# Weight splits, landing places and fill shares in the second layer of a two-layer decoder trunk

## The chip, the cores and the metric

The kernel runs on one core of one Trainium2 chip. The metric is the device time of one execution, in microseconds (us); lower is better. The engines are named as in the profile: PE is TensorE, ACT is ScalarE, DVE is VectorE, POOL is GpSimd, SP is SyncE, which only issues DMAs here.

## The reference

The trunk has two layers over 1024 tokens of width 1024. Each layer computes `LayerNorm(alpha * x + W_out [main * silu(gate); memory * silu(gate)])`. Layer 0's main branch is multi-scale pooling; layer 1's is "forgetting attention" (FoX), which takes nearly half of the time:

```python
def forgetting_attention(u, k, v, cum):       # 16 heads of 64, 1024 x 1024 causal
    logits = q . k * 64 ** -0.5 + (cum[t] - cum[s])   # cum: running sum of log-sigmoid forget gates
    return softmax(where(s <= t, logits, -inf)) . v

def mixer_sublayer(x, mem, w_in, w_mem_kv, w_out, main_fn):
    h = x @ w_in                               # main | memory queries | main gate | memory gate
    y_main, y_mem = main_fn(...), memory_attention(...)     # 4 heads over 256 memory tokens
    y = concat([y_main * silu(g_main), y_mem * silu(g_mem)])
    return y @ w_out                           # w_out is 1536 x 1024
```

Keys, values and forget gates of FoX come from one projection of layer 0's output. Everything is float32 at the borders.

## The kernel before, in words

**Precision.** A float32 product is made of three products of halves: high x high, and the two mixed ones. So every operand is *split*: one engine casts it to the high half, another subtracts to get the low half. `scaled_hi_lo` does it for the projections of layer 1 (high half on ACT, line 171; low half on DVE, line 172, both float16); `hi_lo` does it for the output projection (high half on ACT, line 197; low half on DVE, line 198; a bfloat16 copy of the high half on ACT, line 199). A weight piece first lands in a buffer called `raw` by a DMA on SP's queue.

**Order.** PE runs in the written order (`manual_schedule`). The instructions of the other engines and of the DMA queue are placed by the framework's scheduler, except those that are pinned (`keep_in_program_order`, passed around as `pin`), which keep the written order. Whatever its place, an instruction waits for its data and for the buffer that it writes.

**Start of FoX.** `start_units` computes the values of the first pairs and the forget-gate logits (`v_first`, eight blocks, matmuls on line 845, evacuated on lines 852 to 854), then a long chain of small instructions on DVE (`forget_gates`, lines 863 to 876), and beside it the projections of the first pair (`own`: keys, then queries) and of the second (`following`: keys first). Their matmuls are on line 356, their evacuations on lines 907 and 908. The cumulated gates are matmuls on line 884 that need the end of the chain.

**FoX.** `fox` goes over 16 heads, and in each over `ST` = 8 steps, one step for each tile of 128 queries, longest first, so step k has 128 x (8 - k) keys. A step of 640 keys or more has two parts. The logits are matmuls on line 324 into one of three banks `L`; DVE takes the bank's contents on line 1004 (mask, gates, running minimum); ACT makes exponentials (line 1012); the halves of P are made on ACT (line 1040) and DVE (line 1041); a DMA on SP transposes them to `T` (line 1057), and `values` multiplies them with V (line 1066) `LAG` = 6 steps later. After head 15 come six more steps ("head 16") with values only.

**Fill.** While DVE and ACT work on a step, PE is given other matmuls, the *fill*: the projections of later pairs, and of gates (line 356, with the tanh of a gate on line 372). `fill.pump(columns)` issues some of it. The share of a step is worked out so that steps are of planned lengths: each step's own logits (2 x 128 x (8 - k) columns) are allowed for, corrected by the table `MORE`; steps 1 and 5, where values are computed, by `VALUES`. A share is pumped in two parts (`FRAC` = 0.4, 0.6).

**Evacuating values.** `values` returns a function `out`, which evacuates the bank `O` (ACT line 1086, DVE line 1087) and lets POOL multiply by the gate and SP write to `y1d` in DRAM. `fox` keeps these in `outs`: for one half of a head it is called in the same step, for the other two steps later.

**Output projection.** `OutProj` takes W_out of layer 1 in 24 pieces of 128 x 512. `fetch_two` gets two of them into room that is free anyway, `fetch` gets one into a `raw` buffer; `split` splits in order, fetching first what has not been fetched. Pieces 0 to 7 are fetched during heads 14 and 15; pieces 8 to 11 at the first step of head 16, into `raw`; pieces 12 to 15 and the rest as they are split. Pieces 8 to 13 are split in the last three steps of head 16, pinned; the rest in `rest`. `late_gate` loads the outputs of some pairs back from `y1d` into a buffer `R`, multiplies them by the gate (POOL, line 1113) and writes them again (line 1114); pair 6 is the last. `rest` loads y in pieces (line 631, `T<-y1d`), splits them, and does the products (line 596).

`lines[0]` is a buffer of 16 rows of 1024 float16 numbers per partition; in layer 1 keys and queries of a pair are in its rows 0 to 6 or 8 to 14, by the pair's parity.

Of the kernel before, what the change touches and what calls it, by code (L numbers as in the profile page):

```python
# [9 lines left out]
F32 = mybir.dt.float32  # L10
# [4 lines left out]
AF = mybir.ActivationFunctionType  # L15
ALU = mybir.AluOpType
AX = mybir.AxisListType

P = 128
# [3 lines left out]
ST = S // P  # L23
NH = 512
HEADS = 16
# [12 lines left out]
PSCALE = 2.0 ** 15  # L38
QKSCALE = 2.0 ** -17
VALUES = {1: 39 * P, 5: 15 * P}  # L40
MORE = (-800, 2330, 1130, 410, -310, -70, -1270, -1420)


class Fill:
# [34 lines left out]
def trunk_kernel(ctx, tc, x, xT, memT, win, wk, wv0, wv, wmk, wmv, wout, poolw, pscale, lng, lnb, bforget, out):  # L79
# [90 lines left out]
    def scaled_hi_lo(to, src, sc, pin=lambda ins: ins):  # L170
        pin(nc.scalar.activation(to.hi, src, AF.Copy, scale=sc))  # L171
        pin(nc.vector.scalar_tensor_tensor(to.lo, src, sc, to.hi, ALU.mult, ALU.subtract))
# [32 lines left out]

    roomy = []

    pinned_w = [False]

    def split_w(src_dram, shape, sc=None, r=None):  # L210
        if r is None:
            r = raw(shape)
            nc.sync.dma_start(r, src_dram)
        if sc is not None:
            to = half_of(wt, shape)
            if low[0]:
                gp_scaled_hi_lo(to, r, sc)
            else:
                scaled_hi_lo(to, r, sc, tc.keep_in_program_order if pinned_w[0] else lambda ins: ins)
            return to  # L220
        to = parts_of(wt, shape)
        (gp_hi_lo if low[0] else hi_lo)(to, r)
        return to
# [317 lines left out]
    class OutProj:  # L541
# [8 lines left out]
        def fetch_two(self, land):  # L550

            n = self.n + len(self.raws)
            for j in range(2):
                nc.sync.dma_start(land[:, j, :], wout[self.l, n // 2 % 2, 2 * self.KKS[n // 4] + j])
                self.raws.append(land[:, j, :])

        def fetch(self, upto):

# [233 lines left out]
    X = X1  # L792
    with tc.tile_pool(name="in1", bufs=1) as in1:
# [4 lines left out]
        def land(shape):  # L798
            return sb(list(shape), "B", 10, F32, in1)
# [35 lines left out]
        def v_first():  # L835

            ws = first_ws
            first_vs.extend(vt([P, 2, 2 * ST, 64], F16) for _ in range(2))
            for s in range(ST):
                acc = ps([P, NH], "pj", 2)  # L840
                parts = (1, 2, 0) if s % 2 else (0, 2, 1)
                for i in parts:
                    for kt in range(KT):
                        u, w = three(X[:, kt, s * P : (s + 1) * P], ws[kt // 4][:, kt % 4, :])[i]
                        nc.tensor.matmul(
                            acc[:, :FW], u, w, start=kt == 0 and i == parts[0], stop=kt == KT - 1 and i == parts[2],
                        )
                        yield FW
                for pr in range(2):
                    of = acc[:, pr * P : (pr + 1) * P].rearrange("p (b d) -> p b d", b=2)  # L850
                    hi, lo = (first_vs[pr][:, :, 2 * s + e, :] for e in range(2))
                    nc.scalar.activation(hi, of, AF.Copy, scale=QKSCALE)
                    nc.vector.scalar_tensor_tensor(lo, of, QKSCALE, hi, ALU.mult, ALU.subtract)
                nc.vector.scalar_tensor_tensor(
                    flog[:, s * HEADS : (s + 1) * HEADS], acc[:, 2 * P : FW], un1s[1], bfb, ALU.mult, ALU.add,
                )

        def forget_gates():

# [50 lines left out]
        own_ws = []  # L910

        def own_weights():
            own_ws.extend(split_w(wk[0, pc], [P, 4, P], sws[1]) for pc in range(2))

        def k_units(p):

            own, odd = (lines[0][:, k : k + 2, :] for k in (8 * (p % 2), 8 * (p % 2) + 2))

            def evac(cols, acc):
                halves_out(own[:, 0], own[:, 1], cols, acc, QKSCALE)  # L920
                if cols.stop == S:
                    move((odd, high64, own, high64), (odd, low64, own, high64), (own, high64, own, low64))

            yield from slab(wk[p] if p else own_ws, X, evac, g=1)
            pairs[p] = [[(own[:, 0], own[:, 1]), (odd[:, 0], odd[:, 1])]]

        def q_units(p):

            a, b, c = (lines[0][:, 8 * (p % 2) + k, :] for k in (4, 5, 6))

            def evac(cols, acc):
                halves_out(a, b, cols, acc, -QKSCALE)
                if cols.stop == S:
                    move((c, low64, a, high64), (c, high64, b, high64), (a, high64, b, low64))

            yield from slab(win[1, p], X, evac, g=1)
# [16 lines left out]

        def start_units(own, following):

            pinned_w[0] = True
            yield from v_first()
            gates = forget_gates()
            next(gates)
            yield from islice(own, 58)  # L960
            next(gates)
            yield from islice(own, 9)
            next(gates)
            yield from own
            yield from islice(following, 48)
# [93 lines left out]
        def values(hd, c, o, gs):  # L1059

            v, un, b = pairs[hd // 2][2], unv if hd >= 4 else unv0, hd % 2
            acc = ps([P, NH], "O", 1)
            blocks = [(i, j) for i in range(4 * c, 4 * c + 4) for j in range(i + 1)]

            def add(rows, i, j, e, first, last):
                nc.tensor.matmul(  # L1066
                    acc[rows, (i % 4) * P : (i % 4) * P + P], v[:, b, 2 * j : 2 * j + (1 if e else 2), :].rearrange("p e d -> p (e d)"),
                    pt[hd, i][:, e * (i + 1) + j, :], start=first, stop=last,
                )
# [12 lines left out]
            oc = o[own, c * NH : (c + 1) * NH]  # L1082

            def out():

                nc.scalar.activation(oc, acc[other, :], AF.Copy, scale=un[own])
                nc.vector.scalar_tensor_tensor(oc, acc[own, :], un[own], oc, ALU.mult, ALU.add)
                if b:
                    pair_out(hd // 2, c, o, gs.get(hd // 2))

            return out

        bfb = const.tile([P, HEADS], F32, name="bfb")
        nc.sync.dma_start(bfb, bforget.partition_broadcast(P))
# [20 lines left out]

        def fox(following, out_proj):
            fill, past, fresh = Fill(), [None] * LAG, [None]
            gs, outs = {}, []

            def gate_ahead(pr):  # L1120
                gs[pr] = G()
# [5 lines left out]
            for hd in range(HEADS + 1):  # L1127
# [16 lines left out]
                for i in range(ST if hd < HEADS else LAG):  # L1144
# [1 line left out]
                    last = ST + LAG if hd == HEADS else (hd | 1) * ST + ST  # L1146
                    at = ST if hd == HEADS else hd * ST
                    todo = [VALUES.get(k % ST, 0) if k >= ST else 0 for k in range(at + i, last)]
                    if hd < HEADS:
                        for n, k in enumerate(range(at + i, min(last, HEADS * ST))):  # L1150
                            todo[n] += 2 * P * (ST - k % ST) - MORE[k % ST]
                    part = max(0, (fill.left + sum(todo)) / len(todo) - todo[0])
                    new, split = None, []

# [16 lines left out]
                    if pr == 7:  # L1171
                        step = b * ST + i
                        if step in (0, 1, 5, 11):
                            out_proj.fetch_two(land((P, 2, NH)))
                        if step == 9:
                            lead = out_proj.early(land((P, 4, 2 * P)), parts_of(xy, (P, 4, 2 * P)))
                            next(lead)
                    if hd == HEADS and i == 0:
                        out_proj.fetch(12)
                    if hd < HEADS:  # L1180
                        new = (hd, tile_of, o)
                        fresh[0] = probs(hd, tile_of, R, sums, inverse, behind)
# [9 lines left out]
                        turn(*what)  # L1192
                    older = past[0]
                    if older and older[1] % 4 == 0:
                        outs.append([2 if older[1] else 0, values(older[0], older[1] // 4, older[2], gs)])
                    for one in list(outs):
                        one[0] -= 1
                        if one[0] < 0:
                            one[1]()
                            outs.remove(one)  # L1200
                    if hd == HEADS and i > 2:
                        out_proj.split(4 + 2 * i, True)
                    fill.pump(part * (1 - FRAC[0]))
                    past = past[1:] + [new]
                if b or hd == HEADS:
# [75 lines left out]
```

## Time and profile before

| what | value |
| --- | --- |
| median of 3 runs | 1196.81 us (1196.15 to 1196.82) |
| the profiled execution | 1197.8 us, span 1196.0 us, granted PE clock 0.995 |
| PE busy | 1167.2 us (98% of the span) |
| DVE, ACT, POOL busy | 66%, 58%, 23% |
| first logits of FoX | 651.5 us |
| last logits of FoX | 1047.3 us |

The span is that from the first to the last instruction; the execution's time has 1.8 us around it. In a row of a timeline stand the start, the length, the engine, the line, the operation, the output and inputs by their names in the kernel and shapes, the number of instructions, and in brackets how long the engine sat idle before it and what ended that. Consecutive instructions that are alike are put together. DMA issues are listed under SPq with the time that the issue takes.

### The profile page before, as it was taken

Reading aid. Unit: us, or ns where it says so; the run is one execution under the profiler, and the core shown is the slowest. Engines: PE = TensorE matmul, PEld = TensorE weight load, DVE = VectorE, ACT = ScalarE, POOL = GpSimd, SP = SyncE. Lnnn points to the kernel's source line nnn. Section 1 sums busy time; section 2 is a strip of 40 time slices with the busy share of each in tenths; the row PEclk is TensorE's granted clock in tenths of the full one; section 3 lists DMA queues with packets and bytes.
Section 4 is the critical chain, followed back from the end, with each engine's and each line's share of the span. In section 5 each row is a group of like instructions: output and inputs, shape, how many; then the busy total and the mean of one; then the engine's idle time right before and its main releaser. Section 6 shows DMA issues by size and latency. Waiting matters only on the chain. (4 is left out here: it accounts for less than half of the span.)

```text
span 1196.0 us, 19806 instructions
## 1 busy us (share of the span) xinstructions
PE 1167.2 (98%) x6941; PEld 672.0 (56%) x6941; DVE 786.4 (66%) x1840; ACT 690.0 (58%) x1520; POOL 279.8 (23%) x429
## 2 busy tenths in 40 slices
PE   8999999999999999999999999999999999989996
PEld 5566776555555556556664555555555555445553
DVE  6744675555765557457644888778777887864654
ACT  6568875976563234466422777667766777675210
POOL 4321001310000000010324454554434331730000
PEclk8999999999999999999999999999999999999999
DMA  7576657754285555355724989979897898795430
GB/s 269 167 236 194 167 107 211 245 178 150 90 296 159 142 141 133 96 150 113 222 83 120 193 170 214 208 175 185 191 196 151 159 177 168 197 253 195 164 118 36
DMA packets 286195, 203.88 MB, mean 170 GB/s; under 512 B 224912, under 2 KB 238352, under 8 KB 286096
## 3 DMA queue, kind: packets, MB, share of 16 engines
q1 hardware_dynamic: 279696, 181.59, 60.5%
q0 software_dynamic: 6400, 21.04, 5.6%
q8 instruction: 54, 0.88, 0.3%
q14 instruction: 45, 0.37, 0.1%
HBM read 116.01 MB, written 22.61 MB: 116 GB/s over the span
## 5 line engine op out<-in xcount | busy, mean ns | idle before, releaser
L356 PE MATMUL pj<-A,w 128*128 128x512 f16 (+2 forms) x2896 | 665.1, 383 | 5.6 <-ACT w L171 2.6
L356 PEld LDWEIGHTS <-w 128*128 128x128 f16 (+1 forms) x2560 | 245.1, 98 | 280.7 <-issue 9.5
L1012 ACT ACTIVATE T<-MK,s 128x512 f32<-128x512 f32 x192 | 111.1, 579 | 62.3 <-DVE s L1004 43.0
L1041 DVE SCALAR_TENSOR_TENSOR P<-T,s,P 128x512 f16<-128x512 f32 x192 | 111.6, 613 | 41.4 <-ACT P L1040 39.1
L1040 ACT ACTIVATE P<-T,s 128x512 f16<-128x512 f32 x192 | 102.9, 576 | 55.9 <-issue 23.4
L175 POOL TENSOR_SCALAR B<-B,scales 128x512 f32<-128x512 f32 x54 | 38.8, 728 | 367.3 <-DMA B<-in_win_dram 343.5
L596 PEld LDWEIGHTS <-T 128*128 128x128 bf16 x736 | 70.6, 98 | 91.8 <-issue 7.6
L978 POOL TENSOR_SCALAR_AFFINE_SELECT raw<-R 128x256 f32<-128x256 f32 (+3 forms) x128 | 60.2, 473 | 146.4 <-DVE s L1025 72.9
L198 DVE TENSOR_TENSOR w<-raw,w 128x512 bf16<-128x512 f32 x76 | 54.3, 714 | 54.2 <-ACT w L197 38.1
L324 PE MATMUL L<-A 128*128 128x512 f16 (+3 forms) x384 | 84.5, 326 | 3.5 <-DVE s L1004 3.5
L356 PEld LDWEIGHTS pj<-A,w 128*128 128x128 f32 x352 | 65.3, 188 | 17.1 <-ACT w L197 1.3
L198 DVE TENSOR_TENSOR T<-T,T 128x1024 bf16<-128x1024 f32 x23 | 28.1, 1220 | 67.2 <-PE pj L596 37.6
L324 PEld LDWEIGHTS <-A 128*128 128x128 f16 x384 | 37.5, 98 | 48.3 <-issue 5.5
L177 POOL TENSOR_TENSOR w<-B,w 128x512 f16<-128x512 f32 x54 | 63.3, 1174 | 2.8
L197 ACT CAST w<-raw 128x512 fp32r<-128x512 f32 x78 | 48.0, 615 | 22.8 <-DMA raw<-in_win_dram 9.7
L197 ACT CAST T<-T 128x1024 fp32r<-128x1024 f32 x23 | 24.1, 1047 | 59.7 <-DMA T<-y1d 31.9
L1066 PEld LDWEIGHTS <-V 128*64 128x64 f16 (+1 forms) x1152 | 50.6, 104 | 13.9 <-issue 6.1
L1066 PE MATMUL O<-T,V 128*64 128x128 f16 (+1 forms) x1152 | 57.5, 220 | 0.5 <-DMA T<-P 0.5
L596 PE MATMUL pj<-B,T 128*128 128x512 bf16 (+1 forms) x192 | 53.2, 385 | 0.0
L199 ACT CAST w<-raw 128x512 bf16<-128x512 f32 x80 | 49.4, 618 | 5.5 <-PE pj L356 4.1
L1004 DVE CUSTOM_DVE_ANT_0 MK<-L,R,scales 128x512 f32<-128x512 f32 x64 | 45.4, 709 | 4.7 <-PE L L324 4.6
L596 PE MATMUL L<-B,T 128*128 128x512 bf16 (+1 forms) x168 | 47.3, 394 | 0.8 <-ACT T L199 0.8
(276 smaller groups left out, 1805.8 us busy)
## 6 DMA issues: line engine op xcount, KB each, us to landing
raw<-in_win_dram SPq DMA_DIRECT2D x66, 256.0 KB, 3.6
W<-in_win_dram POOLq DMA_DIRECT2D x48, 256.0 KB, 4.0
raw<-in_wout_dram SPq DMA_DIRECT2D x40, 256.0 KB, 3.2
R<-cumd SPq DMA_DIRECT2D x16, 512.0 KB, 4.6
B<-in_win_dram SPq DMA_DIRECT2D x15, 512.0 KB, 4.8
y0d<-Y SPq DMA_DIRECT2D x12, 512.0 KB, 4.2
T<-y0d SPq DMA_DIRECT2D x12, 512.0 KB, 4.5
A<-A SPq DMA_DIRECT2D x24, 256.0 KB, 4.4
```

Of the source, the lines that this page charges most:

```text
L177: nc.gpsimd.tensor_tensor(to.lo, src, to.hi, ALU.subtract)
L197: pin(nc.scalar.copy(to.hi, src))
L198: pin(nc.vector.tensor_tensor(to.lo, src, to.hi.bitcast(F32), ALU.subtract))
L199: pin((top or nc.scalar.copy)(to.top, src))
L324: nc.tensor.matmul(acc, a, b, start=i == 0, stop=i == len(terms) - 1)
L356: nc.tensor.matmul(accs[n], a[:, k, :], b[:, pc * 4 + k, n * NH : (n + 1) * NH], start=seen[n] == 1, stop=seen[n] == 3 * KT,)
L596: nc.tensor.matmul(accs[a][nh], y, w, start=kt == 8 and i == 0, stop=kt == 7 and i == 2,)
L978: nc.gpsimd.affine_select(C[:, :w], R[:, lo:up], [[-1, w]], ALU.is_ge, -NEG, base=w - P, channel_multiplier=1,)
L1012: nc.scalar.activation(e, p[:, lo:up], AF.Exp, bias=top, scale=-1.0, accum_out=sums[:, n, hd % 2, i : i + 1],)
L1040: nc.scalar.activation(pair[:, lo:up], e, AF.Copy, scale=r)
L1041: nc.vector.scalar_tensor_tensor(pair[:, L + lo : L + up], e, r, pair[:, lo:up], ALU.mult, ALU.subtract)
L1066: nc.tensor.matmul(acc[rows, (i % 4) * P : (i % 4) * P + P], v[:, b, 2 * j : 2 * j + (1 if e else 2), :].rearrange("p e d -> p (e d)"), pt ...
```

## The change

Four things change.

1. The two weight pieces of the first pair's queries are split inside `v_first`, after its blocks 3 and 5, and those of the second pair's keys right behind the chain of forget gates, all pinned. Before, they were split where the projections used them, pinned by a flag that also held for the later splits of `start_units`; those are now free for the scheduler.
2. The table `MORE` and the allowance for the logits are gone: the fill of a pair of heads is given to its steps in equal shares; only steps with values are allowed for.
3. Values are evacuated in the step in which they are computed.
4. Pieces 8 to 15 of W_out are fetched in the last four steps of head 15 in the written order, into rows 0 to 7 of `lines[0]`, two pieces at a time. They are split during five of the steps of head 16, up to pieces 10, 11, 13, 14 and 16, pinned; `raw` buffers first serve piece 16.

```diff
-MORE = (-800, 2330, 1130, 410, -310, -70, -1270, -1420)
...
-                scaled_hi_lo(to, r, sc, tc.keep_in_program_order if pinned_w[0] else lambda ins: ins)
+                scaled_hi_lo(to, r, sc, pin)
...
+                if s in (3, 5):
+                    next_weights(("q", 0), win[1, 0, s // 4])
...
+        def next_weights(what, src):
+            ready[what].append(split_w(src, [P, 4, P], sws[1], pin=tc.keep_in_program_order))
...
-            yield from slab(win[1, p], X, evac, g=1)
+            yield from slab(ready.get(("q", p), win[1, p]), X, evac, g=1)
...
-            pinned_w[0] = True
             yield from v_first()
             gates = forget_gates()
             next(gates)
+            for pc in range(2):
+                next_weights(("k", 1), wk[1, pc])
             yield from islice(own, 58)
...
-                    if hd < HEADS:
-                        for n, k in enumerate(range(at + i, min(last, HEADS * ST))):
-                            todo[n] += 2 * P * (ST - k % ST) - MORE[k % ST]
...
+                        if step > 11:
+                            out_proj.fetch_two([lines[0][:, 2 * step - 24 + j, :].bitcast(F32) for j in range(2)])
...
-                    if hd == HEADS and i == 0:
-                        out_proj.fetch(12)
...
                     if older and older[1] % 4 == 0:
-                        outs.append([2 if older[1] else 0, values(older[0], older[1] // 4, older[2], gs)])
...
+                        values(older[0], older[1] // 4, older[2])
+                        if older[0] % 2:
+                            pair_out(older[0] // 2, older[1] // 4, older[2], gs.get(older[0] // 2))
-                    if hd == HEADS and i > 2:
-                        out_proj.split(4 + 2 * i, True)
+                    if hd == HEADS and i:
+                        out_proj.split((0, 10, 11, 13, 14, 16)[i], True)
```

More of the change, by code (lines that the diff above doesn't have):

```diff
@@ L206, in trunk_kernel, with split_w @@
     roomy = []
-    pinned_w = [False]
-    def split_w(src_dram, shape, sc=None, r=None):
+    def split_w(src_dram, shape, sc=None, r=None, pin=lambda ins: ins):
         if r is None:
@@ L552, in fetch_two @@
             n = self.n + len(self.raws)
-            for j in range(2):
-                nc.sync.dma_start(land[:, j, :], wout[self.l, n // 2 % 2, 2 * self.KKS[n // 4] + j])
-                self.raws.append(land[:, j, :])
+            for j, to in enumerate(land):
+                nc.sync.dma_start(to, wout[self.l, n // 2 % 2, 2 * self.KKS[n // 4] + j])
+                self.raws.append(to)
         def fetch(self, upto):
@@ L908, in halves_out @@
             nc.vector.scalar_tensor_tensor(lo[:, cols], acc, factor, hi[:, cols], ALU.mult, ALU.subtract)
-        own_ws = []
+        ready = {("k", 0): [], ("q", 0): [], ("k", 1): []}
         def own_weights():
-            own_ws.extend(split_w(wk[0, pc], [P, 4, P], sws[1]) for pc in range(2))
+            ready["k", 0].extend(split_w(wk[0, pc], [P, 4, P], sws[1]) for pc in range(2))
+        def next_weights(what, src):
+            ready[what].append(split_w(src, [P, 4, P], sws[1], pin=tc.keep_in_program_order))
         def k_units(p):
@@ L922, in evac @@
                     move((odd, high64, own, high64), (odd, low64, own, high64), (own, high64, own, low64))
-            yield from slab(wk[p] if p else own_ws, X, evac, g=1)
+            yield from slab(ready.get(("k", p), wk[p]), X, evac, g=1)
             pairs[p] = [[(own[:, 0], own[:, 1]), (odd[:, 0], odd[:, 1])]]
@@ L1057, in turn, with values @@
             nc.sync.dma_start_transpose(to[:, :n, :], two[:, : n * P])
-        def values(hd, c, o, gs):
+        def values(hd, c, o):
             v, un, b = pairs[hd // 2][2], unv if hd >= 4 else unv0, hd % 2
@@ L1082, in values @@
             oc = o[own, c * NH : (c + 1) * NH]
[L1084 to L1091, printed above, removed]
+            nc.scalar.activation(oc, acc[other, :], AF.Copy, scale=un[own])
+            nc.vector.scalar_tensor_tensor(oc, acc[own, :], un[own], oc, ALU.mult, ALU.add)
         bfb = const.tile([P, HEADS], F32, name="bfb")
@@ L1117, in fox @@
             fill, past, fresh = Fill(), [None] * LAG, [None]
-            gs, outs = {}, []
+            gs = {}
             def gate_ahead(pr):
@@ L1173, in fox @@
                         if step in (0, 1, 5, 11):
-                            out_proj.fetch_two(land((P, 2, NH)))
+                            two = land((P, 2, NH))
+                            out_proj.fetch_two([two[:, j] for j in range(2)])
+                        if step > 11:
+                            out_proj.fetch_two([lines[0][:, 2 * step - 24 + j, :].bitcast(F32) for j in range(2)])
                         if step == 9:
@@ L1194, in fox @@
                     if older and older[1] % 4 == 0:
-                        outs.append([2 if older[1] else 0, values(older[0], older[1] // 4, older[2], gs)])
[L1196 to L1200, printed above, removed]
-                    if hd == HEADS and i > 2:
-                        out_proj.split(4 + 2 * i, True)
+                        values(older[0], older[1] // 4, older[2])
[3 more added lines that the diff above has]
+                        out_proj.split((0, 10, 11, 13, 14, 16)[i], True)
                     fill.pump(part * (1 - FRAC[0]))
```

## The prediction

> **What bounds the kernel now.** I read the page first, then the windows by stage, the waits of TensorE, and the timelines of each engine around the places that the change touches.
>
> ```profile
> PE 1167.2 (98%) x6941; PEld 672.0 (56%) x6941; DVE 786.4 (66%) x1840; ACT 690.0 (58%) x1520; POOL 279.8 (23%) x429
> ...
> 651.00:1050.00 399.00, 395.52 (x2762) 207.93 (x2761) 317.03 (x917) 279.76 (x665) 189.26 (x291) 1.00 0.88 181
> 1050.00:1075.00 25.00, 21.04 (x148) 11.49 (x147) 14.32 (x25) 17.93 (x32) 7.79 (x8) 1.00 0.94 250
> ...
> PE L L324 <- DVE s L1004: 3.5, 6, 1.1
> ```
>
> TensorE (PE) is busy for 1167.2 of 1196.0 us, and no part of the change removes a matmul. So the change is worth what it does to PE's idle time. The two window rows (PE, weight load, DVE, ACT and POOL busy, then clock, DMA share and GB/s) say where that idle time is: 3.5 us in the 399 us of the forgetting attention (FoX), all of it the six waits of the last row, against 4.0 us in the 25 us after it, where the output projection begins. The third place is the start of FoX, between the first values and the first logits:
>
> ```profile
> 625.55 1.90 PE L356 MATMUL pj<-A,w 128*128 128x512 f16 x8 [1.30 <-ACT w L171]
> 629.18 5.79 PE L356 MATMUL pj<-A,w 128*128 128x512 f16 x26 [1.73 <-DVE w L172]
> 634.80 0.38 PE L884 MATMUL O<-G,G 128*128 128x128 f32 x2
> 641.09 10.53 PE L356 MATMUL pj<-A,w 128*128 128x512 f16 x48 [1.30 <-ACT w L171]
> ...
> 624.78 1.32 ACT L171 ACTIVATE w<-raw,scales 128x512 f16<-128x512 f32 x2
> 640.32 1.32 ACT L171 ACTIVATE w<-raw,scales 128x512 f16<-128x512 f32 x2
> ...
> 616.64 0.29 DVE L853 SCALAR_TENSOR_TENSOR V<-pj,V 128x128 f16<-128x128 f32 x1 [1.71 <-ACT V L852]
> 619.42 0.29 DVE L853 SCALAR_TENSOR_TENSOR V<-pj,V 128x128 f16<-128x128 f32 x1 [1.71 <-ACT V L852]
> 628.37 0.75 DVE L172 SCALAR_TENSOR_TENSOR w<-raw,scales,w 128x512 f16<-128x512 f32 x1
> 631.66 0.29 DVE L876 TENSOR_TENSOR G<-G 128x128 f32<-128x128 f32 x1
> 641.07 2.66 DVE L172 SCALAR_TENSOR_TENSOR w<-raw,scales,w 128x512 f16<-128x512 f32 x2
> ...
> 600.87 0.51 SPq L213 DMA_DIRECT2D raw<-in_wk_dram  x1
> ```
>
> PE waits three times for weights that are being split: 1.30 us for the high half of the own queries' first piece, 1.73 us for a low half that DVE makes in the middle of the forget gates, 1.30 us for the second keys. The last row is the last of the five loads of these pieces: they were issued 24 us earlier, so only the splits are late.
>
> **Part 1: weights split ahead.** Two queries' pieces are split after the values' blocks 3 and 5, the two pieces of the second keys right behind the forget gates. Added: nothing, the same four ACT instructions (0.66 us each) and four DVE instructions (0.75) stand earlier. In the values' stage both engines have room: DVE idles 1.71 us ahead of a block's first evacuation (rows 616.64 and 619.42, a block apart: 2.8 us), and ACT, which starts each pair, about as long. A late evacuation there would cost PE at most the 0.75 us of one split. The forget gates lose two of DVE's splits, so their last row ends at about 630.5 in place of 631.95; PE, which no longer waits 3.03 us, needs them at 634.80 - 3.03 = 631.8. The margin is about 1 us, and that chain is what is late next. The second keys' splits fill ACT from about 624 and DVE behind the gates; PE takes them at 641.09 - 4.33 = 636.8. All three waits go: **-4.3 us**, bounds -4.4 and 0 (the gates late by as much as the waits that went).
>
> **Part 2: equal shares.** Without the table and the allowance for logits, step k of a head gets 256(8-k) - 1152 - MORE[k] columns of fill more than before. Added up to the end of steps 0 to 7 that is +1696, +6, -740, -1022, -840, -1154, -524 and 0. A matmul has 512 columns and takes 0.22 us (48 in 10.53 us above), so step 1's logits come 0.73 us later, those of steps 3 to 7 come 0.2 to 0.5 us earlier, and a head as a whole takes as long.
>
> ```profile
> 705.45 0.38 PE L324 MATMUL L<-A 128*128 128x256 f16 x2 [0.59 <-DVE s L1004]
> ...
> 972.89 0.48 PE L324 MATMUL L<-A 128*128 128x384 f16 x2 [0.66 <-DVE s L1004]
> ...
> 1025.84 0.48 PE L324 MATMUL L<-A 128*128 128x384 f16 x2 [1.14 <-DVE s L1004]
> ```
>
> Five of the six waits stand before the 384-column part of step 1 (the last two rows, and three under 0.5 us); 0.73 us of delay ends four of them and leaves 0.41 us of the largest. The first row is step 3, which comes 0.32 us earlier and so waits about 0.9. From 3.5 us some 1.3 are left, and a few other heads will show a short wait at step 3: **-2.0 us**. The bounds are -3.5 (all waits go) and +3 (DVE, busy 317 of 399 us, is late at step 3 in most heads).
>
> **Part 3: values evacuated at once.** No instruction goes or comes. The compiled order shows that few of these evacuations change place on ACT and DVE; the next use of the one O bank by PE comes four steps later. I take 0; 0.3 us either way.
>
> **Part 4: W_out pieces 8 to 15 in stream rows.** They are 256 KB DMAs on SP's queue, in the compiled order one at the end of layer 0 and seven between the transposes of heads 12 to 14; the DMA share there is 0.88, the transposes have six steps of lag, and I take 0 for them (0 to +1). The raw buffers that held pieces 8 to 15 now receive pieces 16 to 19, at the queue places of 8 to 11, and here the compiled order has a trap.
>
> ```profile
> 1051.64 0.98 PE L596 MATMUL pj<-B,B 128*128 128x512 f32 x2
> 1053.83 2.47 PE L1066 MATMUL O<-T,V 128*64 128x128 f16 x52 [0.52 <-DMA T<-P]
> 1066.30 0.61 PE L596 MATMUL L<-B,T 128*128 128x512 bf16 x2 [0.81 <-ACT T L199]
> 1067.69 0.38 PE L596 MATMUL pj<-MK,T 128*128 128x512 bf16 x1 [0.35 <-DVE MK L198]
> 1068.73 0.38 PE L596 MATMUL pj<-MK,T 128*128 128x512 bf16 x1 [0.66 <-DVE MK L198]
> 1070.75 0.38 PE L596 MATMUL L<-w,T 128*128 128x512 bf16 x1 [1.42 <-DVE w L198]
> 1071.88 0.38 PE L596 MATMUL L<-w,T 128*128 128x512 bf16 x1
> ...
> 1047.08 0.58 ACT L1040 ACTIVATE P<-T,s 128x384 f16<-128x384 f32 x1
> 1047.56 0.68 ACT L372 ACTIVATE G<-pj,scales 128x512 f32<-128x512 f32 x1
> 1052.31 0.68 ACT L372 ACTIVATE G<-pj,scales 128x512 f32<-128x512 f32 x1
> 1056.34 0.68 ACT L1086 ACTIVATE G<-O,scales 64x512 f32<-64x512 f32 x1 [3.35 <-PE O L1066]
> 1057.05 0.62 ACT L197 CAST B<-raw 128x512 fp32r<-128x512 f32 x1
> ...
> 1053.79 1.41 POOL L1113 TENSOR_TENSOR R<-R,G 128x256 f32<-128x256 f32 x2 [2.15 <-DVE G L373]
> ...
> 1046.75 1.53 SPq L562 DMA_DIRECT2D raw<-in_wout_dram  x1
> 1048.38 0.39 SPq L1114 DMA_DIRECT2D y1d<-R  x1
> ...
> y1d<-R SPq DMA_DIRECT2D x1, 512.0 KB, 4.3
> ...
> y1d<-R SPq DMA_DIRECT2D x1, 512.0 KB, 6.5
> ...
> 1070.00 0.69 DVE L198 TENSOR_TENSOR w<-raw,w 128x512 bf16<-128x512 f32 x1
> ```
>
> What it removes: the waits of PE for splits of pieces 8 to 15 and their data, 0.81 + 0.35 + 0.66 + 1.42 us in these rows, and the 0.52 us ahead of the values.
>
> What it adds: the high halves of pieces 16 to 19 are casts without a fixed place, and the scheduler put them early on ACT. The first stands directly behind the P half of row 1047.08, where the gate's tanh of row 1047.56 stood. It writes the R buffer that gate 5's outputs still occupy, until the DMA of row 1048.38 has landed, 4.3 us after its issue (the first of the two rows with KB and us to landing; the other is the next such write): 1052.7. ACT would be free at 1047.6, so it stands for 5.1 us. Queued behind: that tanh, the last two tiles' exponentials, the casts of W_out pieces 6 and 7, those of 17 to 19, and gate 6's second tanh (before at 1052.31). That an engine does not pass over a waiting instruction is what rows 1056.34 and 1057.05 show: the cast of a piece fetched at 1046.75 stood behind an evacuation that waited 3.35 us. The Trainium skill's "Perfetto Trace Analysis" (section on the Tensor Engine instruction) says so too: ACT, DVE and GpSimd are strict FIFO. By that rule the term below stands; could ACT go past the cast, the tail would gain 3.8 us.
>
> Step by step, on the clock of before: cast to 1053.2; tanh, exponentials, P halves and casts (each as long as in before, some 3.9 us) put piece 7's cast at about 1057.1, and PE, which used it at about 1051.9 (row 1051.64), stands there 5.3 us; of that 0.8 us replaces idle time it had (0.52 for T<-P and the rest), so +4.5. The second tanh follows the casts of pieces 18 and 19, at 1060.5 for 1052.3; DVE 0.7 us, POOL 1.4 us (row 1053.79), and the write of gate 6's outputs is issued at about 1062.6 and lands about 1067.1. DVE's low half of piece 16 waits for that, and ahead of it on DVE is nothing, but behind it are the evacuation of O, seven low halves at 0.69 (row 1070.00) and the split of the first T of the tail. From 1067.1 they take DVE to about 1074.6, the pieces 12 and 13 behind them to 1078.1. PE then has 35 of that block's 48 matmuls left at 1078.15; before it had 37 left at 1071.88. So +6.27 - 2 x 0.22 = **+5.9 us**, with the removed waits already in. Bounds: +4 (the write lands 2 us sooner) and +8 (both landings nearer to the 6.5 us of the other row). By the same reckoning the loads of pieces 20 to 23 then land ahead of PE's use.
>
> The sum on this execution (1197.8 us, 1.8 of it outside the span of 1196.0): -4.3 - 2.0 + 0 + 5.9 = -0.4, so 1197.4. It ran 1.0 us over the median of 1196.81, so I forecast **1196.4 us**.
>
> The Trainium skill's page "DMA: Bandwidth & Descriptors" (Anatomy of one DMA) has 2.0 us plus bytes over 436 GB/s, which is 3.2 us for 512 KB where the row has 4.3. By it ACT would stand 1.1 us less and the sum would be 1195.3; at a DMA share of 0.94 I keep the row.
>
> **The rivals.** (a) FoX loses, slower: DVE has no room at step 3. If the 0.3 us that its second part comes earlier turns into waiting in half of the 16 heads, that is +2.4 us, and the 3.5 us stay: 4.4 over my sum, 1200.8. It decides when DVE ends the part that held the bank less than 0.3 us ahead of PE in most heads. For it: 79% busy DVE and one wait there already; against: only one of 16 heads waits at step 3 now.
> (b) The tail's block is longer: both landings take 6.5 us instead of 4.3 and 4.5. ACT and DVE each lose 2 us more: tail +10.3, 1200.8. Against it: eight pieces fewer share the DMA engines there.
> (c) The block costs little, faster: gate 5's write lands before ACT arrives, or the scheduler's place is harmless because PE has other work in front. Then the tail is between -3.8 and +2: 1186.7 to 1192.5. For it: the pieces do come early; against: the rows give the landing 5.1 us after ACT is free.
> (d) Part 1 doesn't do what it says: the forget gates or the moves of queries are late by what the splits were. Then the start is 0 and the time 1200.7.
>
> **How the numbers follow.** My forecast has 0.38 (its own range 1194.4 to 1198.8), (a) 0.20, (b) 0.13, (c) 0.23, (d) 0.06. A difference under 0.2%, 2.4 us, is about what a measurement of this kernel cannot tell from none. Faster is (c) and a little of the forecast's low end, 0.24; slower is (a), (b) and (d) without their low ends, 0.38; the rest 0.38. The range reaches to 1190.5, over half of (c), and to 1202.0 for (a) and (b) with the unknown of part 4's early DMAs.
>
> **What would show it.** In the changed profile: no wait for w by L356 between 619 and 647; the 128x384 logits of step 1 without waits, and one or more new waits at step 3; an ACT cast from raw behind P with about 5 us of idle time ahead of it near 1043 to 1048, PE idle about 5 us before a matmul on B; PE busy at the end of the first products about 6 us later than the start's gain would put it. I am wrong if that cast finds its buffer free, or if waits of L324 add up to more than 4 us.

## The result: 0.26% slower, and the profile after

The changed kernel took 1200.37 us (median of 22 runs, 1197.56 to 1204.84), the kernel before, measured beside it, 1197.26 us (22 runs, 1193.60 to 1200.97). The ratio is 1.0026, 95% interval 1.0016 to 1.0036: slower by 3.1 us. Two later series of the same two kernels gave 0.9999 (0.9985 to 1.0012) and 1.0019 (1.0004 to 1.0033). The profiled execution of the changed kernel is, by chance, its fastest one: 1197.56 us, with a span of 1195.8 us against 1196.0. So its total says nothing, but its stages do. First the two window rows, FoX and the 25 us behind it, and PE's waits in FoX:

```profile
PE 1168.1 (98%) x6941; PEld 672.9 (56%) x6941; DVE 784.4 (66%) x1840; ACT 689.3 (58%) x1520; POOL 281.4 (24%) x429
...
651.00:1050.00 399.00, 392.57 (x2745) 206.78 (x2743) 314.03 (x912) 278.07 (x663) 185.80 (x285) 1.00 0.91 191
1050.00:1075.00 25.00, 20.50 (x140) 11.13 (x141) 15.94 (x24) 18.79 (x33) 6.63 (x7) 0.93 0.40 121
...
PE L L321 <- DVE s L1007: 4.9, 7, 1.5
```

PE's waits in FoX went from 3.5 to 4.9 us, where the forecast had 1.5. The DMA share behind FoX fell from 0.94 to 0.40 (eight pieces of W_out now come earlier), but PE is no busier there, and its granted clock is 0.93. Next, PE at the start of FoX, with the forget gates' last row on DVE:

```profile
617.91 12.68 PE L353 MATMUL pj<-A,w 128*128 128x512 f16 x58
630.81 0.46 PE L883 MATMUL O<-G,G 128*128 128x128 f32 x2 [0.21 <-DVE G L875]
634.64 11.60 PE L353 MATMUL pj<-A,w 128*128 128x512 f16 x53
646.08 1.03 PE L321 MATMUL L<-A 128*128 128x512 f16 x4
...
630.00 0.66 DVE L875 TENSOR_TENSOR G<-G 128x128 f32<-128x128 f32 x1
```

The three waits for weights are gone: 58 matmuls in one piece. Only 0.21 us of waiting for the forget gates has come. The tail, on ACT, PE, DVE and SP's queue:

```profile
1042.95 0.58 ACT L1043 ACTIVATE P<-T,s 128x384 f16<-128x384 f32 x1
1046.55 0.62 ACT L196 CAST R<-raw 128x512 fp32r<-128x512 f32 x1 [3.02 <-DMA y1d<-R]
1047.08 0.68 ACT L369 ACTIVATE G<-pj,scales 128x512 f32<-128x512 f32 x1
1050.61 0.60 ACT L196 CAST B<-B 128x512 fp32r<-128x512 f32 x1
...
1051.26 0.80 PE L593 MATMUL pj<-B,B 128*128 128x512 f32 x1 [1.76 <-ACT B L196]
1053.27 2.96 PE L1069 MATMUL O<-T,V 128*64 128x128 f16 x52
1069.86 0.38 PE L593 MATMUL pj<-MK,T 128*128 128x512 bf16 x1 [0.64 <-DVE MK L197]
1072.13 0.38 PE L593 MATMUL pj<-MK,T 128*128 128x512 bf16 x1 [1.46 <-DVE MK L197]
...
1059.67 0.69 DVE L197 TENSOR_TENSOR R<-raw,R 128x512 bf16<-128x512 f32 x1 [4.94 <-DMA y1d<-R]
...
1041.97 0.39 SPq L1110 DMA_DIRECT2D y1d<-R  x1
1056.25 0.33 SPq L1110 DMA_DIRECT2D y1d<-R  x1
```

The cast that writes R stands on ACT for 3.02 us until the DMA that reads R has landed, PE then waits for the cast of a piece into B, and the low half of piece 16 stands on DVE for 4.94 us in front of the others. The values' 52 matmuls, 2.47 us long before, took 2.96.

**Stages.** Every profiled execution can be cut at four starts on PE: the first matmul of the first values (line 845 before), the first logits, the last logits, and the first product of the output projection into a bank T. What follows that takes 115.9 us in every one. In us:

| execution | until first values | start | FoX | tail |
| --- | --- | --- | --- | --- |
| before | 595.5 | 55.9 | 395.9 | 32.7 |
| changed | 595.2 | 50.9 | 397.4 | 36.5 |
| changed_again | 599.0 | 51.3 | 397.5 | 38.4 |
| changed_third | 595.6 | 51.3 | 397.6 | 36.7 |
| weights_only | 597.3 | 51.6 | 395.9 | 32.2 |
| equal_only | 599.7 | 56.0 | 396.4 | 31.6 |
| values_only | 595.3 | 56.3 | 396.2 | 31.5 |
| wout_only | 597.6 | 56.0 | 396.1 | 37.4 |
| table_back | 595.2 | 51.3 | 396.1 | 37.8 |
| other_slots | 597.0 | 51.7 | 397.5 | 39.5 |
| pinned_rest | 599.1 | 51.6 | 397.5 | 29.6 |
| all_mended | 596.2 | 51.8 | 395.1 | 31.3 |
| mended_again | 596.3 | 51.5 | 395.9 | 30.3 |
| no_landing | 598.9 | 51.6 | 396.0 | 31.7 |
| no_landing_again | 596.2 | 51.3 | 395.9 | 31.2 |
| step1_later | 596.2 | 51.6 | 397.4 | 31.0 |
| steps3_earlier | 597.4 | 51.2 | 395.1 | 30.1 |

The first column, which no edit aims at, varies by 4.5 us and makes most of the scatter of the totals. Start and FoX repeat within 0.8 us for the same code. The tail of before was its longest: the six executions with W_out fetched as before (before, weights_only, equal_only, values_only and both of no_landing) have a mean of 31.8 us, the three of the changed kernel 37.2.

### The profile page after: what moved, and what is told of

Read it like the earlier page. It is cut to its first block, busy times and chain, and to the rows that moved or that the text cites. A ratio compares the mean times of both kernels' runs of the same rounds, so it can differ in the third digit from the quotient of the medians.

```text
span 1195.8 us, 19786 instructions
## 1 busy us (share of the span) xinstructions
PE 1168.1 (98%) x6941; PEld 672.9 (56%) x6941; DVE 784.4 (66%) x1840; ACT 689.3 (58%) x1520; POOL 281.4 (24%) x429
## 5 line engine op out<-in xcount | busy, mean ns | idle before, releaser
L1043 ACT ACTIVATE P<-T,s 128x512 f16<-128x512 f32 x192 | 103.0, 576 | 53.5 <-issue 28.9
L197 DVE TENSOR_TENSOR w<-raw,w 128x512 bf16<-128x512 f32 x74 | 51.8, 701 | 51.6 <-ACT w L196 35.5
L321 PEld LDWEIGHTS <-A 128*128 128x128 f16 x384 | 37.4, 98 | 48.3 <-issue 6.9
```

The costliest lines, as they stand in the source:

```text
L197: pin(nc.vector.tensor_tensor(to.lo, src, to.hi.bitcast(F32), ALU.subtract))
L321: nc.tensor.matmul(acc, a, b, start=i == 0, stop=i == len(terms) - 1)
L1043: nc.scalar.activation(pair[:, lo:up], e, AF.Copy, scale=r)
```

## The experiments

**One part at a time: weights_only, equal_only, wout_only, values_only.** Each is the kernel before with one part's hunks of the change.

```diff
 weights_only:  + next_weights(("q", 0), ...) after blocks 3 and 5;  + next_weights(("k", 1), ...) behind the gates
 equal_only:    - todo[n] += 2 * P * (ST - k % ST) - MORE[k % ST]
 wout_only:     + fetch_two into lines[0] at steps 12 to 15;  - out_proj.fetch(12);  + split((0, 10, 11, 13, 14, 16)[i], True)
 values_only:   - outs.append(...);  + values(...) and pair_out(...) at once
```

> The kernel before with part 1 alone (queries' and second keys' weights split ahead). Theory 1 (the three waits at the start, 4.3 us, were pure idle time and nothing takes their place): 4 to 6 us faster than before, no wait for w between 600 and 647 us, FoX as long as before. Rival (the forget gates or the moves of queries take their place): less than 2 us faster, a new wait before the first logits.

Measured: 1194.06 us against 1198.86, ratio 0.9960 (0.9947 to 0.9974), 4.8 us faster by the medians. The start is 51.6 us for 55.9, 4.3 us shorter, FoX unchanged. Theory 1 holds.

> The kernel before with equal shares alone (no table, no allowance for logits). Theory 2 (step 3's second part now reaches PE before DVE has freed the bank, in about half of the heads): waits of L for s of 5 to 6 us in FoX, at the 256-column part of step 3, and 1 to 3 us slower than before. Rival, the forecast (step 1's waits go, step 3 keeps one): 2 us faster.

Measured: 1199.83 us, ratio 1.0003 (0.9989 to 1.0018). FoX is 0.5 us longer, less than the 0.8 us by which FoX repeats; the waits of L are 3.9 us in six waits, five of them at step 3's 256-column part. In place, theory 2; in size, between the two: no gain, and no loss clear of the scatter.

> The kernel before with part 4 alone (pieces 8 to 15 in stream rows). Theory 3 (the cast of piece 16 stands on ACT until the DMA that reads its R buffer has landed): 4 to 7 us slower than before, an ACT cast into R with 3 to 5 us of idle time ahead of it and a stall of PE of 2 us or more on piece 7. Rival (the early pieces are the gain, the cast waits little): 2 to 4 us faster.

Measured: 1205.06 us, ratio 1.0052 (1.0034 to 1.0070), 6.2 us slower. ACT and PE of this execution:

```profile
1053.07 0.62 ACT L197 CAST R<-raw 128x512 fp32r<-128x512 f32 x1 [2.91 <-DMA y1d<-R]
...
1055.06 0.72 PE L596 MATMUL pj<-V,B 128*128 128x512 f32 x2 [1.37 <-DVE G L373]
1058.18 0.79 PE L596 MATMUL pj<-B,B 128*128 128x512 f32 x1 [2.17 <-ACT B L197]
1060.19 4.25 PE L1066 MATMUL O<-T,V 128*64 128x128 f16 x52
```

The same cast stands 2.91 us, PE waits first for the gate behind it, then for B. Theory 3 holds.

> The kernel before with part 3 alone (values evacuated in the step that computes them). Forecast: no instruction goes or comes, 0 us, FoX 369.4 us from the first logits to head 15's first, within 0.3. Rival (the earlier evacuation takes DVE's time ahead of step 3's logits, which is why the changed kernel waits 5.0 us there and equal shares alone only 3.9): FoX 0.5 us or more longer.

Measured: 1197.29 us, ratio 0.9992 (0.9977 to 1.0007); FoX 0.2 us longer. The forecast's 0 holds; evacuating at once costs little by itself. The rival is wrong for part 3 alone. Beside equal shares FoX was 397.5 us (pinned_rest) where equal shares alone had 396.4; those two kernels differ in parts 1 and 4 as well, which alone gave 395.9 and 396.1, so the two parts seem to cost more together than apart.

**The late casts pinned: pinned_rest.**

```diff
                 if splits:
-                    self.split(splits.pop(0))
+                    self.split(splits.pop(0), X is None)
```

> The changed kernel, and the splits of pieces 16 to 23 in the rest of the output projection pinned to the written order. Theory 3 (the casts' place is what costs): the wait ahead of an R cast is gone, PE has no stall on pieces 6 and 7 and at most 1 us in the first block of products, 5 to 8 us faster than the changed kernel, so 2 to 5 us faster than before. Rival (the loads, or the lower clock after idle time from other causes): the tail stays within 2 us of that of the changed kernel.

Measured: 1193.66 us against 1198.86, ratio 0.9959 (0.9943 to 0.9974). Where the changed kernel has the R cast, ACT goes on; PE's waits in its tail:

```profile
1047.79 0.58 ACT L1043 ACTIVATE P<-T,s 128x384 f16<-128x384 f32 x1
1048.27 0.68 ACT L369 ACTIVATE G<-pj,scales 128x512 f32<-128x512 f32 x1
...
PE pj L593 <- DVE MK L197: 0.8, 1, 0.8
PE pj L593 <- ACT B L196: 0.5, 1, 0.5
```

The tail is 29.6 us, and the whole is 5.2 us faster than before. One edit, to the place of these splits on ACT and DVE, takes away the whole loss of part 4; SP's queue has its loads, transposes and writes in the same order up to the write of gate 6's outputs. That the place is what costs is shown.

**What the early cast waits for: other_slots.**

```diff
-[("w", 0), ("MK", 4), ("R", 2), ("V", 4), ("PG", 0), ("B", 10)]
+[("w", 0), ("MK", 4), ("V", 4), ("R", 2), ("PG", 0), ("B", 10)]
```

> The changed kernel with the slots of pieces 16/17 and 18/19 exchanged (V first, then R), nothing pinned: the cast of piece 16 is as early on ACT but needs only its own load; the cast that writes R is piece 18's, six instructions later. Theory 3 in its exact form (the buffer of gate 5's outputs is what is waited for): the idle time ahead of the piece 16 cast falls from 3.0 us to under 1, PE's stall on piece 7 to under 1 us, the tail 33 to 35 us instead of 36.5 or more. Rival (any early cast of pieces 16 to 19 costs that much, since their loads are late too): the tail stays at 36 us or more.

Measured: 1202.64 us, ratio 1.0023 (1.0010 to 1.0035), tail 39.5 us.

```profile
1048.09 0.62 ACT L196 CAST V<-raw 128x512 fp32r<-128x512 f32 x1 [4.64 <-DMA raw<-in_wout_dram]
...
1055.32 0.62 ACT L196 CAST R<-raw 128x512 fp32r<-128x512 f32 x1 [1.08 <-DMA raw<-in_wout_dram]
```

My exact form of theory 3 fell, its rival held. Without the R buffer the cast stood even longer, for its own load, and the order had put it still further ahead, in front of a P half of 512 columns. So the buffer is one of two things that are late; the fault is the early place.

**The changed kernel again: changed_again, changed_third** (no edit).

> The changed kernel once more, for the spread. Its first profiled execution was no longer than that of before, its median 3.1 us longer. Theory 4 (the stages repeat, and only the first layer's length and the granted clock after the stall differ between executions): FoX from the first logits to head 15's first within 0.3 us of 370.7, the start 50.9 to 51.7 us, the tail from the last logits to the second group of products at least 36.5 us and up to 2 us longer, with a granted clock under 0.9 in the stretch behind the stall; total 2 to 5 us over before. Rival (the profiled execution was typical and the median comes from one long stage elsewhere): a stage longer by 2 us or more outside the tail.

Measured: 1199.92 us against 1199.52, ratio 0.9999 (0.9985 to 1.0012). The profiled one took 1203.86: start and FoX as expected, a first column longer by 3.8 us than that of the first profile, and a tail of 38.4 us. A window of PE behind the stall in this execution, then the same window of before (the clock is third from the end):

```profile
1056.00:1060.00 4.00, 4.00 (x40) 2.98 (x41) 1.59 (x3) 1.97 (x4) 0.52 (x1) 0.57 0.46 114
```

```profile
1056.00:1060.00 4.00, 4.00 (x24) 2.20 (x22) 2.55 (x4) 3.63 (x7) 2.11 (x2) 1.00 1.25 159
```

Theory 4 holds for the stages; the total of the series was below what it gave.

> The changed kernel, third series. By its stages (start -4.7, FoX +1.5, tail +3.8 to +5.7 against the profiled execution of before) it is 0.5 to 2.5 us slower than before; the first layer's length adds scatter of a few us to single executions. A ratio over 1.004 or under 0.998 would say that the stages do not tell all.

Measured: 1200.43 us against 1198.38, ratio 1.0019 (1.0004 to 1.0033), inside the expected 0.5 to 2.5 us.

**The table back: table_back; both losses mended: all_mended, mended_again.**

```diff
 table_back:   + MORE and todo[n] += 2 * P * (ST - k % ST) - MORE[k % ST], on the changed kernel
 all_mended:   table_back, and self.split(splits.pop(0), X is None)
```

> The changed kernel with the table and the allowance for logits back (part 2 undone; parts 1, 3 and 4 stay). Theory 2 (equal shares cost 1.3 us of FoX): FoX back to 369.4 us from the first logits to head 15's first, waits of L for s at 3.5 us, 1 to 2 us faster than the changed kernel. Rival (shares are worth nothing and what FoX lost comes from the values' evacuation at once): FoX stays at 370.7 us. The R cast stays early in this order, so the tail keeps its stall, 36 to 38 us.

Measured: 1200.79 us, ratio 1.0006 (0.9993 to 1.0019). FoX is back (396.1 us, waits of L 3.6), the tail 37.8 us. Both stages as expected; the total, beside the changed kernel's 1199.92 on the same chip, doesn't show the 1 to 2 us. In this order the R cast stood 4.24 us, and the tail is 0.6 us over the changed kernel's mean; that is a part of what is missing, and the rest is not explained.

> The changed kernel with the table back and the splits of pieces 16 to 23 pinned: parts 1, 3 and 4 with both losses mended. If the terms add (start -4.3, FoX 0, tail -3.2 against before): 6 to 8 us faster than before and 1 to 2 us faster than the changed kernel with pinned splits alone. If the shares are worth nothing: equal to that one, 4.5 to 5.5 us faster than before.

Measured: 1191.71 us, ratio 0.9927 (0.9912 to 0.9942), 7.8 us faster than before, where pinned_rest was 5.2 and the added terms give 7.5.

> The mended kernel (weights ahead, values at once, table back, pieces 8 to 15 in stream rows, last splits pinned) once more, on the chip of the others. If its stages tell all: 6 to 7 us faster than before and 1.5 us faster than the one without early landing. If the medians of the first series do: 8 to 9 us and 4 us.

Measured: 1192.40 us, ratio 0.9948 (0.9932 to 0.9963). This series gives 6.0 us, the first gave 7.8; both intervals hold 0.9932 to 0.9942, some 7 to 8 us faster than before. It beats both kernels and is, with steps3_earlier and no_landing_again below, among the fastest versions tried.

**Is the landing worth anything: no_landing, no_landing_again.**

```diff
 on all_mended:  - fetch_two into lines[0];  + out_proj.fetch(12);  + if hd == HEADS and i > 2: out_proj.split(4 + 2 * i, True)
```

> The mended kernel (weights ahead, values at once, table back, last splits pinned) with W_out fetched as before: part 4's early landing taken out. If the landing rows are what gains in the tail (3.8 us of waits for the splits of pieces 8 to 15): 4 to 5 us faster than before and a tail of about 32.2 us, 3 to 4 us slower than the mended kernel. Rival (pinning the last splits gives the gain by itself): within 1 us of the mended kernel, tail 31.3 us or less.

Measured: 1195.20 us, ratio 0.9967 (0.9954 to 0.9980), 3.6 us faster than before.

> The mended kernel without the early landing once more, on the same chip: 4 to 5 us faster than before by its first series and by its stages; beside the mended kernel this gives the worth of the landing rows once nothing stands in their way, 0.5 to 1.4 us by the stages, 4 us by the medians of the first series.

Measured: 1192.34 us, ratio 0.9948 (0.9932 to 0.9964), beside 1192.40 for the kernel with the landing. The tails are 31.7 and 31.2 us against 31.3 and 30.3. By the stages the landing rows are worth 0.7 us in the mean, by these two totals nothing; the 4 us between the medians of the first series, which ran on different chips, did not come again.

**Which half of the equal shares costs: step1_later, steps3_earlier.** Both are all_mended with another table.

```diff
-MORE = (-800, 2330, 1130, 410, -310, -70, -1270, -1420)
+MORE = (896, 640, 1124, 410, -310, -70, -1270, -1420)      # step1_later
+MORE = (-800, 2330, 390, 128, -128, -384, -640, -896)      # steps3_earlier
```

> The mended kernel with a table that keeps only the part of the equal shares that the forecast counted on: +1696 columns of fill in step 0, -1690 in step 1, -6 in step 2, all later steps as before. Theory 2 in its exact form (equal shares lost by step 3's logits coming earlier, not by step 1's coming later): the waits at the 384-column part of step 1 go, no new ones at step 3, waits of L for s at 1 us or less, 1 to 2 us faster than the mended kernel. Rival (a later step 1 makes DVE late at step 3 by itself): waits at step 3 as in the changed kernel, FoX 370 us or more.

Measured: 1194.37 us, ratio 0.9965 (0.9953 to 0.9978); FoX 397.4 us, 1.5 to 2.3 over all_mended's two.

```profile
PE L L322 <- DVE s L1008: 4.4, 8, 0.7
```

Six of the eight waits are at step 3's 256-column part, though nothing moved there. My theory fell, its rival is right.

> The mended kernel with a table that keeps only the other part of the equal shares: steps 0 and 1 as before, 740 columns less fill in step 2 and then as in equal shares, so that steps 3 to 7 get their logits 0.2 to 0.5 us earlier and step 1's stay where they were. Theory 2 in its first form (the earlier step 3 is what costs): waits at the 256-column part of step 3 in six or seven heads, waits of L for s of 5 us or more, FoX from the first to the last logits 396.5 us or more. Theory 5 (DVE idles while step 1's logits come late and is then late at step 3): DVE's idle time before the first part's instruction as in the mended kernel, 4.7 us, at most two waits at step 3, FoX within 1 us of the mended kernel's 395.1.

Measured: 1191.15 us, ratio 0.9937 (0.9921 to 0.9953), FoX 395.1 us, one short wait at step 3 (0.21 us), the others at step 1. The earlier steps 3 to 7 cost nothing. DVE's idle time ahead of a step's first part did rise, against theory 5's sign for it:

```profile
L1008 DVE CUSTOM_DVE_ANT_0 MK<-L,R,scales 128x512 f32<-128x512 f32 x64 | 45.4, 709 | 7.5 <-PE L L322 7.4
```

A better sign is the margin at the part that waits: from the end of the instruction on line 1008 (1004 before) that frees the bank, step 2's first part, to PE's first matmul into it, step 3's second part. Its median over the 16 heads is 0.89 us in before and mended_again, 0.93 in steps3_earlier, and 0.10 in step1_later, where step 1 comes 0.64 us later in the mean. In the changed kernel and in equal_only the median is 0.64 and 0.65, but the heads spread, up to 2.38 us. What tells there is how many of the 16 heads have a margin of 0.11 us or less: one in before and in steps3_earlier, five in equal_only, seven in the changed kernel, ten in step1_later.

## Why the prediction was wrong, point by point

**Part 1, -4.3 us: right.** Measured 4.6 to 5.0 us in the stage of the changed kernel, 4.3 alone. The forget gates were late by 0.21 us where I had left them 1 us. Their last row ended at 630.66, close to the forecast's 630.5, though some rows of DVE's chain ran longer than before (the last 0.66 us for 0.29); but PE came to them at 630.60, not at 631.8. It began the stage 0.4 us earlier in this execution, and a wait of 0.57 us ahead of the matmuls on line 845, which before had and I had not counted, was gone too.

**Part 2, -2.0 us: the step that failed.** Measured +1.5 to +1.7 us in the changed kernel (FoX 397.4 to 397.6 for 395.9), and all but 0.2 us of it gone with the table back (396.1). The waits of L are 4.9 us, over the 4 us that the prediction gave as a sign of being wrong. Three of them, and DVE ahead of the second:

```profile
699.47 0.38 PE L321 MATMUL L<-A 128*128 128x256 f16 x2 [0.68 <-DVE s L1007]
722.85 0.38 PE L321 MATMUL L<-A 128*128 128x256 f16 x2 [0.52 <-DVE s L1007]
825.44 0.38 PE L321 MATMUL L<-A 128*128 128x256 f16 x2 [0.44 <-DVE s L1007]
...
721.39 0.73 DVE L1087 SCALAR_TENSOR_TENSOR G<-O,scales,G 64x512 f32<-64x512 f32 x1
722.05 0.73 DVE L1007 CUSTOM_DVE_ANT_0 MK<-L,R,scales 128x512 f32<-128x512 f32 x1
```

"0.73 us of delay ends four of them" was right: of five waits at step 1 one is left. The sentence behind it was wrong: I let "a few other heads" show a short wait at step 3 because it comes 0.32 us earlier, and took the later step 1 as free. In fact six heads wait there, 0.44 to 1.49 us each. The earlier step 3 is not the reason (steps3_earlier), and a later step 1 is enough by itself to bring six such waits (step1_later). In step1_later the way is plain: DVE begins step 1's first part 5.2 us after the first logits of a head for 4.5 in before, ends step 2's first part, which holds the bank that step 3 needs, at 10.8 for 10.2, and the margin is used up.

In the changed kernel that is not the whole of it. There DVE begins step 1 at 4.5 us, as in before, and ends step 2's first part at 10.0, so in the mean it isn't late. But in nine of the 16 heads an evacuation of values (line 1087, 0.73 to 0.76 us) stands on DVE between step 1's and step 2's first part, as in the last two rows, and all seven heads without margin are among these nine. Before has it in six heads, and one of them has no margin. So the place of this evacuation in DVE's order belongs to the loss, and my reading for part 3, that few evacuations change place, was wrong here: the heads that have it are others for nine of the 16. In four of the six waits it is longer than the wait. How much comes from its place and how much from the later step 1 was not tried, and stays open.

The waits in the page show where the margin is zero, not where it is 0.9; I read only the waits. Of the rivals, (a) had the place right and the reason wrong, and its 1200.8 us came nearest; (b) to (d) did not come about.

**Part 3, 0: right alone** (0.2 us of FoX). Beside equal shares it may cost up to 1.0 us (pinned_rest against equal_only, which differ in more); parts 2 and 3 together, without the others, were not tried. That 1.0 us is a part of the +1.5 above, not beside it.

**Part 4, +5.9 us: right in mechanism, and near in size partly by luck.** (The terms as written, 6.27 - 2 x 0.22, give 5.8.) The three tails average 37.2 us, 5.4 over the six with the old fetch; against the one profile that I had, +3.8, +5.7 and +4.0. The path was the one forecast: ACT behind the R cast, the later write of R, DVE's low halves one after another, and PE at row 1072.13 waiting for the last of them. Two terms were off in opposite directions. The landings were sooner: ACT stood 3.0 us for 5.1, since the write of R was issued 1.6 us before ACT came free (1041.97, and 1042.95 + 0.58) and not 0.8 us after, and the later one landed 3.4 us after its issue (1056.25, and DVE's start at 1059.67), not 4.5. Against that, DVE took 12.4 us from there to the low half that ended PE's last wait (1072.08), not 11.0. On the profile that I had, this leaves +3.8. That the mean is nearer to 5.9 is luck: the tail of before was the longest of its six, and changed_again lost 1.6 us to a lower clock, below, for which the forecast had no term.

The Trainium skill's "Perfetto Trace Analysis" (Tensor Engine instruction) states a strict order for ACT and DVE; the trace agrees, as ACT ran nothing in the 3.02 us that the cast stood. The Trainium skill's "DMA: Bandwidth & Descriptors" (Anatomy of one DMA) has a fit for DMAs issued by GpSimd. The estimate by it for that 512 KB write is 3.2 us, and the two here, on SP's queue, took 4.6 (1041.97 to the cast at 1046.55) and 3.4.

**The sum.** -4.3 - 2.0 + 0 + 5.9 became -4.8 + 1.6 + 5.4 = +2.2 us, with means of 51.1 us for the start and 397.5 for FoX. The three series gave +3.1, +0.4 and +2.1. My forecast of -0.4 had the right two large terms; the sign of the third made the difference.

## What to carry to other kernels

When work on the main engine is moved to end a wait, look at the margin of the next few hand-overs on the engine behind it, and at the order of its instructions, not only at the waits: a delay that is harmless at one step can be paid two steps later. When data are fetched earlier, look at what the freed buffers and free-floating instructions do: here the scheduler used the new room to put casts ahead of work that PE needed, and pinning them took 7.6 us off the tail (37.2 to 29.6), where the early loads themselves were worth about 0.7. And a single profiled execution is compared by stages that repeat, not by its total.

## What the runs showed of the hardware

The granted clock of PE fell after the stall in the tail. In all six executions with early casts (changed, its two repeats, wout_only, table_back, other_slots) it fell to between 0.50 and 0.71 in a window of 4 us behind it; of the others only weights_only showed such a fall (0.57), behind two waits of 0.66 and 1.42 us. The values' 52 matmuls are 2.47 us long at full clock, 2.96 in the changed kernel, 4.25 in wout_only. Idle time alone doesn't decide it: before had PE busy for 1.8 of 4 us at 1068 and kept 1.00. Windows of the changed kernel, then of weights_only, then of changed_again with PE's wait ahead of it:

```profile
1050.00:1053.00 3.00, 1.74 (x4) 1.16 (x4) 1.84 (x7) 2.04 (x6) 0.48 (x1) 0.65 0.49 127
1053.00:1057.00 4.00, 4.00 (x57) 3.51 (x57) 0.69 (x1) 1.72 (x4) 1.41 (x2) 0.83 0.27 53
...
1066.00:1070.00 4.00, 3.72 (x10) 1.36 (x10) 2.97 (x4) 4.00 (x7) 1.95 (x2) 0.57 0.46 163
...
1076.82 0.59 PE L593 MATMUL pj<-MK,T 128*128 128x512 bf16 x1 [1.46 <-DVE MK L197]
1076.00:1080.00 4.00, 3.18 (x8) 1.17 (x8) 1.90 (x2) 0.93 (x2) 0.22 (x1) 0.58 0.74 239
```

What decides it stays open. Whether it costs time depends on what PE waits for next. In the three executions of the changed kernel PE ran behind the stall into the wait for DVE's low halves (row 1072.13 of the first). From the last logits to the end of that wait it took 28.7, 29.0 and 28.9 us, whatever the clock ahead of it had been, and from there to the first product into T 7.8, 9.4 and 7.8. So the slower matmuls ahead of the wait seem to have cost nothing there; the 1.6 us that changed_again has more stand behind it, where its clock fell a second time.
